# A four-layer diffusion trunk on one core: sublayer ends in two parts of feature quarters, weight conversions on VectorE, three tiles handed over

## The chip, the cores and the metric

The kernel runs on one core of one Trainium2 chip. The metric is the device time of one execution in microseconds (us), as the median of three runs. All traces are of that one core.

The core's engines work side by side, each through its own list of instructions in a fixed order: TensorE (PE: matrix products and transposes; its weight loads are shown as PEld), VectorE (DVE), ScalarE (ACT), GpSimd (POOL) and SyncE (SP, which issues most transfers). An instruction waits for the semaphores of what it reads and writes; everything behind it on its engine waits with it.

## What is computed

Four layers, each a token mixer (differential attention `da`, neighbourhood attention `na`, grouped-query attention `gq`, Hyena convolution `hy`) and a squared-ReLU MLP. After each of these eight sublayers the residual stream is updated, normalised and modulated for the next one:

```python
def layer_norm(x, g, b):
    xf = x.astype(jnp.float32)
    mu = jnp.mean(xf, axis=-1, keepdims=True)
    var = jnp.mean(jnp.square(xf - mu), axis=-1, keepdims=True)
    return ((xf - mu) * lax.rsqrt(var + LN_EPS) * g + b).astype(x.dtype)

def modulate(x, shift, scale):
    return x * (1.0 + scale) + shift
```

A sublayer adds `gate * (o @ w)` to ALPHA times the stream, applies `layer_norm`, and hands `modulate(...)` of it to the next. There are 128 context tokens and 512 latent tokens, 1024 features, all in float32.

## The kernel before

The 640 tokens are five tiles of 128: tile 0 holds the context, tiles 1 to 4 the latents. Products are made in three passes (`mm3`): a float32 operand is split into a high part `hh` or `hl[:, 0]` that TensorE takes at its fast rate and a low part (`hl`), and high x high, high x low and low x high are added up. So each weight of 128 x 1024 is converted after it arrives: a cast on ACT (L451) and a subtraction (L453) on DVE. Converted weights live in five buffers, raw ones in three; `wget` takes the next one of the stream and keeps the conversion a given number ahead.

The change is about the seven **ends** at which a sublayer passes over into the next (`sublayer_end`; the eighth, after the last MLP, has a branch of its own). An end has five tiles by four feature quarters of closing products, 20 groups of 12 matmuls of 128 x 256. Of each group DVE multiplies the result by the gate (`gtmp`, L655), and DVE or POOL adds it to the stream `r` (L662). When a tile has its four quarters, `ln_norm` takes statistics (two `bn_stats` L687, `bn_aggr` L689), the square root on ACT (L691), reciprocal and factor on DVE (L692, L693), and normalises the tile on ACT (L698; half of tile 4 on DVE, L700). `ln_out` then transposes it on TensorE (8 transposes L724 into `lnt`) and makes the next sublayer's input: the first half of the features by four modulations on ACT (L730), the second by a multiplication and an addition on DVE (L732, L733), each then cast to `hh` on ACT (L734) and subtracted to `hl` (L736; on POOL for the first half of tiles below LT = 3, else DVE).

The order within an end: tile by tile, all four quarters of a tile one after the other, the norm of tile t - 1 between the two halves of tile t, and `ln_out` two tiles behind. The last two `ln_out` are left **pending**; the next sublayer begins with products on tiles already made and calls `flush` between them (the MLP's `w1_first` after each of its first four products of 256 tokens; the mixers' `lead`, which takes two query and key projections and then the values; `hy_in_gen`). Thereafter `settle` scales the residual stream (L742, L743 on POOL and DVE). The four closing weights must all be there from the start of an end, so those of the next sublayer are converted during it: one at tile 3, two at tile 4 and one behind. Of these three have their subtraction on POOL, since `relieve` is set from tile 4 until the last `flush`.

The order of the instructions on each engine follows a scheduler's priorities, except where `manual_schedule` keeps the order in which the code is written.

Of the kernel before, what the change touches and what calls it, by code (L numbers as in the profile page):

```python
# [18 lines left out]
P = 128  # L19
D = 1024  # L20
# [37 lines left out]
LT = 3  # L58
# [13 lines left out]
# ---------------------------------------------------------------- host layout and shape constants  # L72
# [206 lines left out]
# ---------------------------------------------------------------- device program  # L279
class Trunk:  # L280
# [4 lines left out]
    def __init__(self, ctx, tc, a, outs, layers):  # L285
# [13 lines left out]
        self.relieve = False  # L299
# [9 lines left out]
        self.early = {}  # L309

    # ---- small helpers
# [33 lines left out]
    # ---- weight stream  # L345
# [28 lines left out]
    def side_keys(self, n):  # L374
        """filter work of the MLP of the layer at n: entries after each unit of w1, and after each of w2"""
# [19 lines left out]
    def head_order(l):  # L395
        """order of the projections: values of a group of four heads, queries and keys of a pair"""
# [39 lines left out]
    def w_convert(self, upto):  # L436
        while self.w_cv < min(upto, len(self.wlist)):
# [34 lines left out]
    # ---- products in three passes  # L472
# [6 lines left out]
    def span_a(self, ps, t, c0, c1):  # L479
        """feature-major product of one unit with tokens c0 to c1; yields now and then"""  # L480
# [6 lines left out]
    # ---- adaLN  # L487
# [30 lines left out]
    def ada_load(self, l, step):  # L518
        """weights of one step: 128 rows (or the bias row) of two neighbouring modulations"""
# [10 lines left out]
    def ada_step(self, raw, l, m, k):  # L530
        """128 rows of a modulation weight times their factors, added up row by row; the sum over partitions ends it"""
# [39 lines left out]
    def ada_gen(self, l, ahead, p0, p1):  # L571
        """pairs p0 to p1 of modulations of a layer; one step per yield, its weights loaded `ahead` steps before"""
# [44 lines left out]
    def load_ln(self, l, j, last=False):  # L617
        """gain and bias of a LayerNorm on all partitions, scaled for the residual stream"""
# [9 lines left out]
    def spill(self):  # L628
        """residual stream to DRAM, to be fetched by restore"""
# [13 lines left out]
    def restore(self):  # L643
        """residual stream back on chip; its tiles are finished by ready"""
# [4 lines left out]
    def residual(self, ps, t, q, quick=False):  # L649
        """r[t, quarter q] += gate * ps"""  # L650
# [13 lines left out]
    # ---- LayerNorm and modulation  # L664
# [80 lines left out]
    def ln_residual(self):  # L745
        for t in range(NT):
            self.ln_tile(t)
# [1482 lines left out]
```

## Time and profile before

| | us |
|---|---|
| median of 3 runs (1 core) | 3496.15 |
| the three runs | 3494.53, 3496.15, 3499.4 |
| span of the profiled execution | 3487.9 |
| busy PE / DVE / ACT / POOL | 3324.3 / 2600.0 / 1512.3 / 1003.6 |

The profiled execution is, by its span, 8.2 us shorter than the median of the runs. A row of a timeline gives start, duration, engine, line, operation and tile names, and in brackets how long the engine was idle before it and what ended that. A row of stretches gives each engine's busy time and, under PEclk, the TensorE clock that was granted, as a share of full speed. Matmul rows are pipelined, so a row's length is more than its share of the time.

### The profile page before, as it was taken

The page shows a single profiled execution, that of the slowest core. Times are in us where ns is not written, and L with a number is a line of the kernel's source. Part 1 is how long each engine was busy: PE and PEld are TensorE (multiplying, and loading weights), DVE is VectorE, ACT ScalarE, POOL GpSimd, SP SyncE. Part 2 cuts the span into 40 slices and gives each one's busy share as a digit, 9 for nine tenths or more (in the row PEclk, how much of TensorE's full clock was granted, in tenths as well). Part 3 has the DMA queues.
Part 4 walks back from the last instruction along what each step waited for, and adds up shares of the span by engine and source line. Part 5 has one row for each costly group of instructions (what it writes and reads, how often), then busy time and mean ns, then how long its engine had stood idle before and what let it go on. Part 6 is the DMA issues. An engine that isn't in the chain of part 4 may idle for free. (4 is left out here: it accounts for less than half of the span.)

```text
span 3487.9 us, 63715 instructions
## 1 busy us (share of the span) xinstructions
PE 3324.3 (95%) x25288; PEld 3183.9 (91%) x25288; DVE 2600.0 (75%) x4691; ACT 1512.3 (43%) x2700; POOL 1003.6 (29%) x961
## 2 busy tenths in 40 slices
PE   8998999999999989999998999999998999999998
PEld 6878889998999889999988889999998998999998
DVE  4777888788676678777688878777859888945457
ACT  3555453333356654433335665333324333432322
POOL 0333334334354453122252014232334112500002
PEclk9999999999999999999999999999999999999999
DMA  7343134545242324555412112545523224222221
GB/s 271 122 133 108 49 129 165 171 166 175 82 130 77 104 75 158 187 169 197 143 60 69 31 53 94 184 152 182 164 93 123 81 81 152 88 91 79 85 75 54
DMA packets 157644, 418.97 MB, mean 120 GB/s; under 512 B 19550, under 2 KB 29414, under 8 KB 154270
## 3 DMA queue, kind: packets, MB, share of 16 engines
q1 hardware_dynamic: 157344, 414.88, 35.8%
q8 instruction: 199, 3.26, 0.4%
q14 instruction: 101, 0.83, 0.1%
HBM read 371.20 MB, written 34.05 MB: 116 GB/s over the span
## 5 line engine op out<-in xcount | busy, mean ns | idle before, releaser
L662 POOL TENSOR_TENSOR r<-r,gtmp 128x256 f32<-128x256 f32 x444 | 437.8, 999 | 1127.6 <-DVE gtmp L655 1097.3
L453 DVE TENSOR_TENSOR hl<-raw,hl 128x1024 fp32r<-128x1024 f32 x390 | 506.6, 1301 | 322.1 <-ACT hl L451 320.6
L475 PE MATMUL w<-hl,ff 128*128 128x256 f32 x2560 | 716.0, 280 | 7.2 <-DVE gtmp L655 7.1
L476 PE MATMUL w<-hl,ff 128*128 128x256 f32 x2560 | 715.2, 279 | 2.5 <-DVE hl L453 2.4
L477 PE MATMUL w<-hl,ff 128*128 128x256 f32 x2560 | 713.9, 279 | 0.0
L451 ACT CAST hl<-raw 128x1024 fp32r<-128x1024 f32 x411 | 430.2, 1048 | 638.3 <-PE w L477 508.9
L475 PE MATMUL w<-hh,hl 128*128 128x320 f32 (+2 forms) x2048 | 637.7, 312 | 0.2
L476 PE MATMUL w<-hl,hl 128*128 128x320 f32 (+2 forms) x2048 | 634.9, 310 | 1.8 <-DVE hl L736 1.8
L477 PE MATMUL w<-hh,hl 128*128 128x320 f32 (+2 forms) x2048 | 634.3, 310 | 0.0
L475 PEld LDWEIGHTS w<-hl,ff 128*128 128x128 f32 x2560 | 481.0, 188 | 12.1 <-DVE gtmp L655 9.9
L476 PEld LDWEIGHTS w<-hl,ff 128*128 128x128 f32 x2560 | 480.9, 188 | 5.0 <-DVE hl L453 3.3
L477 PEld LDWEIGHTS w<-hl,ff 128*128 128x128 f32 x2560 | 479.9, 187 | 0.0
L543 DVE SCALAR_TENSOR_TENSOR ada<-adaw,sil,ada 128x512 f32<-128x512 f32 x504 | 388.2, 802 | 88.2 <-DMA adaw<-in_ada_w 80.5
L475 PEld LDWEIGHTS w<-hh,hl 128*128 128x128 f32 x2048 | 387.2, 189 | 13.8 <-issue 8.4
L476 PEld LDWEIGHTS w<-hl,hl 128*128 128x128 f32 x2048 | 387.2, 189 | 3.1 <-DVE hl L736 3.0
L477 PEld LDWEIGHTS w<-hh,hl 128*128 128x128 f32 x2048 | 387.0, 189 | 0.8 <-issue 0.8
L655 DVE TENSOR_TENSOR gtmp<-w,gate 128x256 f32<-128x256 f32 x640 | 261.1, 415 | 162.4 <-PE w L477 152.1
L874 ACT ACTIVATE fx<-w 128x640 f32<-128x640 f32 (+2 forms) x136 | 91.6, 673 | 454.2 <-PE w L477 435.3
L475 PE MATMUL qk<-hh,hl 128*128 128x320 f32 (+2 forms) x672 | 216.5, 322 | 6.7 <-DVE gtmp L655 3.9
L476 PE MATMUL qk<-hl,hl 128*128 128x320 f32 (+2 forms) x672 | 211.0, 314 | 0.0
L477 PE MATMUL qk<-hh,hl 128*128 128x320 f32 (+2 forms) x672 | 211.0, 314 | 0.0
L475 PE MATMUL wo<-hl,oh 128*128 128x256 f32 x640 | 184.0, 288 | 8.9 <-DVE gtmp L655 5.8
(344 smaller groups left out, 7132.4 us busy)
## 6 DMA issues: line engine op xcount, KB each, us to landing
raw<-in_w SPq DMA_DIRECT2D x256, 512.0 KB
adaw<-in_ada_w SPq DMA_DIRECT2D x288, 256.0 KB
adaw<-in_ada_w SPq DMA_DIRECT2D x16, 1024.0 KB
raw<-ab_d SPq DMA_DIRECT2D x32, 512.0 KB
raw<-in_hy_in SPq DMA_DIRECT2D x24, 512.0 KB
adaw<-in_ada_s SPq DMA_DIRECT2D x8, 1024.0 KB
raw<-in_da_qk SPq DMA_DIRECT2D x16, 512.0 KB
gate<-gate_d SPq DMA_DIRECT2D x32, 256.0 KB
```

What stands on the lines that cost most here:

```text
L451: self.nc.scalar.copy(t[:, 0], raw)
L453: sub(t[:, 1], raw, t[:, 0].bitcast(F32))
L475: mm(ps, w[0], x[0], start=start, stop=False)
L476: mm(ps, w[0], x[1], start=False, stop=False)
L477: mm(ps, w[1], x[0], start=False, stop=stop)
L543: nc.vector.scalar_tensor_tensor(out=y, in0=raw[h], scalar=x, in1=y, op0=ALU.mult, op1=ALU.add)
L655: nc.vector.tensor_mul(tmp, ps, self.gate[2 * s + q // 2][:, (q % 2) * 256:(q % 2) * 256 + 256])
L662: eng.tensor_add(rv, rv, tmp)
L874: nc.scalar.activation(x, src, AF.Relu)
```

## The change

`sublayer_end` gets the next weight by a function (`unit`), one quarter at a time, and works in two parts. Part 1 goes quarter by quarter: quarter 0 for all five tiles, then quarter 1 for all five, where the statistics of a tile's first half (`ln_half`) follow. The weights of the coming quarters and of the next sublayer are converted meanwhile, up to four ahead. Part 2 goes tile by tile through quarters 2 and 3, with each tile's norm right behind it; `ln_out` of tiles 0 and 1 follows tiles 2 and 3; three tiles stay pending in place of two. From part 2 to `settle`, PE and POOL keep the written order. The conversions' subtractions are always on DVE, the first half of tile 2 is subtracted on DVE (LT = 2), the second half of each tile is modulated by four instructions of 128 x 128 in place of two of 128 x 512, and the residual stream is scaled from tile 4 on. `lead` hands over after its first, second and third product; the Hyena opening hands over a third time. In `gq`, four multiplications for the rotary tables go from DVE ahead of the opening to ACT behind it. Docstrings fall away. The core of the diff:

```diff
-LT = 3
+LT = 2
@@ w_convert
-            sub = self.nc.gpsimd.tensor_sub if self.relieve else self.nc.vector.tensor_sub
-            sub(t[:, 1], raw, t[:, 0].bitcast(F32))
+            self.nc.vector.tensor_sub(t[:, 1], raw, t[:, 0].bitcast(F32))
@@ ln_norm
+            st = self.st.pop(t) if t in self.st else self.ln_half(t, 0)
+            self.ln_half(t, 1, st)
@@ ln_out
-                nc.vector.tensor_mul(x, pss[h], self.gs[:, f, s:s + 1].to_broadcast([P, 4, P]))
-                nc.vector.tensor_add(x, x, self.bs[:, f, s:s + 1].to_broadcast([P, 4, P]))
+                for k in range(4):
+                    nc.vector.tensor_scalar(out=x[:, k], in0=pss[h][:, k], scalar1=self.gs[:, 4 + k, s:s + 1], scalar2=self.bs[:, 4 + k, s:s + 1], op0=ALU.mult, op1=ALU.add)
@@ ln_residual
-        for t in range(NT):
+        for t in (NT - 1,) + tuple(range(NT - 1)):
@@ sublayer_end
-        for t in range(NT):
-            group(t, 0)
-            if t == 1:
-                while self.ln_raw:
...
-            if t == 3:
-                self.w_convert(self.wi + 1)
-            if t == NT - 1:
-                self.relieve = True
-                self.w_convert(self.wi + 3)
-            if t > 0:
-                self.ln_norm(t - 1)
-            group(t, 1)
-            if t == NT - 1:
-                self.ln_norm(t)
-            if t > 1:
+        self.st = {}
+        for q in range(2):
+            u = unit(q, 4)
+            for t in range(NT):
+                group(u, t, q, False)
...
+                if q == 1:
+                    self.st[t] = self.ln_half(t, 0)
+        self.man.enter_context(self.tc.manual_schedule(engines={mybir.EngineType.PE, mybir.EngineType.Pool}))
+        us = {2: unit(2, 4)}
+        us[3] = unit(3, 3)
+        for t in range(NT):
+            for q in (2, 3):
+                group(us[q], t, q, t > 2)
+            self.ln_norm(t)
+            if t in (2, 3):
                 self.ln_out(t - 2)
         self.w_convert(self.wi + 4)
-        self.pending = [lambda t=t: self.ln_out(t) for t in (NT - 2, NT - 1)]
+        self.pending = [lambda t=t: self.ln_out(t) for t in range(2, NT)]
@@ v_gen
-            if led and t > 2:
+            if led and t > 1:
@@ lead
-        for g in tiles + [None, None, values]:
+        for g in (tiles[0], None, tiles[1], None, values, None):
@@ gq
-                    nc.vector.tensor_scalar(out=t[s], in0=cs[s], scalar1=gg[:, 2 * i + s:2 * i + s + 1], scalar2=None, op0=ALU.mult)
...
             self.lead(ks, values)
+                    nc.scalar.activation(t[s], cs[s], AF.Copy, scale=gg[:, 2 * i + s:2 * i + s + 1])
@@ hy_in_gen
                     yield from self.span_a(early[1], early[0], c0, c1)
+                    self.flush(1)
```

The last argument of `group` puts the additions to `r` on DVE: before for tile 4, now for tiles 3 and 4.

Where instructions come to stand is shown at the first end (`da` to its MLP). Names carry numbers: `r_3495` is the stream, `gtmp` a gated product, `st`, `mv` and `rs` the statistics, the mean and variance and the factors of one tile, `hl_` with `raw_` a weight. **VectorE at the first norms.** Before, `mv_4305` and `rs_4307` are of tile 0 and `st_4376` is of tile 1:

```order
L655 TENSOR_TENSOR gtmp_4263<-wo_4250,gate_3716 128x256
L662 TENSOR_TENSOR r_3495<-r_3495,gtmp_4263 128x256
L687 BN_STATS st_4302<-r_3495 128x6
L655 TENSOR_TENSOR gtmp_4279<-wo_4266,gate_3503 128x256
L689 BN_AGGR mv_4305<-st_4302 128x2
L655 TENSOR_TENSOR gtmp_4295<-wo_4282,gate_3503 128x256
L687 BN_STATS st_4376<-r_3495 128x6
L692 RECIPROCAL rs_4307<-rs_4307 128x1
L655 TENSOR_TENSOR gtmp_4325<-wo_4312,gate_3718 128x256
L693 SCALAR_TENSOR_TENSOR rs_4307<-mv_4305,rs_4307 128x1
```

Now `st_4307` and `rs_4423` are of tile 0, `st_4325` is of tile 1, `hl_4383` is a weight of the next sublayer:

```order
L452 TENSOR_TENSOR hl_4383<-raw_4198,hl_4383 128x1024
L654 TENSOR_TENSOR gtmp_4401<-w_4388,gate_3716 128x256
L654 TENSOR_TENSOR gtmp_4417<-w_4404,gate_3716 128x256
L661 TENSOR_TENSOR r_3495<-r_3495,gtmp_4417 128x256
L683 BN_STATS st_4307<-r_3495 128x6
L654 TENSOR_TENSOR gtmp_4441<-w_4428,gate_3718 128x256
L698 BN_AGGR mv_4421<-st_4307 128x2
L654 TENSOR_TENSOR gtmp_4457<-w_4444,gate_3718 128x256
L683 BN_STATS st_4325<-r_3495 128x6
L701 RECIPROCAL rs_4423<-rs_4423 128x1
L654 TENSOR_TENSOR gtmp_4481<-w_4468,gate_3718 128x256
L702 SCALAR_TENSOR_TENSOR rs_4423<-mv_4421,rs_4423 128x1
```

In both the reciprocal of tile 0 stands behind statistics of tile 1: before behind those of its first half, now behind those of its last quarters; a weight's subtraction stands ahead of the first gated product of part 2.

**ScalarE at the end of the last tile.** Before, `rs_4579` is of tile 3, `rs_4621` of tile 4, `h_4524` and `h_4531` are the halves of tile 1, `h_4637` and `h_4644` those of tile 2:

```order
L698 ACTIVATE r_3495<-r_3495,rs_4477 128x1024
L730 ACTIVATE h_4524<-lnt_4514,bs,gs 128x128 x4
L734 CAST hh_4200<-h_4524 128x4x128
L451 CAST hl_4568<-raw_4188 128x1024
L734 CAST hh_4200<-h_4531 128x4x128
L451 CAST hl_4571<-raw_4190 128x1024
L691 ACTIVATE rs_4579<-mv_4577,epst 128x1
L451 CAST hl_4649<-raw_4195 128x1024
L698 ACTIVATE r_3495<-r_3495,rs_4579 128x1024
L730 ACTIVATE h_4637<-lnt_4627,bs,gs 128x128 x4
L451 CAST hl_4786<-raw_4658 128x1024
L691 ACTIVATE rs_4621<-mv_4619,epst 128x1
```

Now `h_4582` and `h_4589` are the halves of tile 1, `h_4518` the first half of tile 0, `rs_4503` is of tile 2, `rs_4567` of tile 3:

```order
L707 ACTIVATE r_3495<-r_3495,rs_4503 128x1024
L743 CAST hh_4189<-h_4518 128x4x128
L739 ACTIVATE h_4582<-lnt_4572,bs,gs 128x128 x3
L700 ACTIVATE rs_4567<-mv_4565,epst 128x1
L739 ACTIVATE h_4582<-lnt_4572,bs,gs 128x128
L451 CAST hl_4637<-raw_4200 128x1024
L707 ACTIVATE r_3495<-r_3495,rs_4567 128x1024
L743 CAST hh_4189<-h_4582 128x4x128
L743 CAST hh_4189<-h_4589 128x4x128
L451 CAST hl_4798<-raw_4289 128x1024
L700 ACTIVATE rs_4631<-mv_4629,epst 128x1
L707 ACTIVATE r_3495<-r_3495,rs_4631 128x512
```

Four casts of weights stood here and two do now; the first of them and the norm of tile 3 stand between tile 1's modulation and its cast.

**GpSimd over the same stretch.** Before, the last two additions and what follows them:

```order
L662 TENSOR_TENSOR r_3495<-r_3495,gtmp_4495 128x256
L736 TENSOR_TENSOR hl_4201<-h_4524,hh_4200 128x4x128
L453 TENSOR_TENSOR hl_4568<-raw_4188,hl_4568 128x1024
L453 TENSOR_TENSOR hl_4571<-raw_4190,hl_4571 128x1024
L736 TENSOR_TENSOR hl_4201<-h_4637,hh_4200 128x4x128
L453 TENSOR_TENSOR hl_4649<-raw_4195,hl_4649 128x1024
L742 TENSOR_TENSOR r_3495<-r_3495,ln_g_4110 128x512
```

Now:

```order
L661 TENSOR_TENSOR r_3495<-r_3495,gtmp_4481 128x256
L745 TENSOR_TENSOR hl_4190<-h_4518,hh_4189 128x4x128
L745 TENSOR_TENSOR hl_4190<-h_4582,hh_4189 128x4x128
L751 TENSOR_TENSOR r_3495<-r_3495,ln_g_4110 128x512
L752 TENSOR_TENSOR r_3495<-r_3495,ln_b_4112 128x512
```

The three subtractions of weights and the one of tile 2 are gone.

## Rows read from the trace of the kernel before

**Rows 1.** The page's first part: busy time, share of the span, instructions of each engine.

```profile
PE 3324.3 (95%) x25288; PEld 3183.9 (91%) x25288; DVE 2600.0 (75%) x4691; ACT 1512.3 (43%) x2700; POOL 1003.6 (29%) x961
```

**Rows 2.** Stretches of 52 us, one around each end: length, busy times, granted clock, DMA.

```profile
418.00:470.00 52.00, 46.25 (x345) 45.17 (x344) 47.48 (x68) 31.76 (x57) 35.02 (x25) 0.93 0.17 52
...
1775.00:1827.00 52.00, 43.78 (x331) 42.30 (x331) 47.18 (x70) 24.80 (x48) 33.96 (x25) 0.90 0.17 58
...
2989.00:3041.00 52.00, 46.11 (x345) 44.84 (x344) 47.94 (x68) 29.31 (x53) 34.79 (x25) 0.93 0.12 42
sum 364.00, PE 317.63 PEld 308.80 DVE 330.88 ACT 201.24 POOL 244.43; mean PE 45.38 PEld 44.11 DVE 47.27 ACT 28.75 POOL 34.92
```

**Rows 3.** Waits of PE from 418 to 470: total us, times, longest.

```profile
PE lnt L724 <- ACT r L698: 5.0, 2, 4.4
```

**Rows 4.** Waits of PE from 1775 to 1827, the end of the second MLP.

```profile
PE v L475 <- DVE h L732: 2.6, 1, 2.6
PE qk L475 <- DVE rs L693: 2.5, 1, 2.5
```

**Rows 5.** Timeline of PE at the first end; x8 are eight transposes.

```profile
425.76 1.03 PE L724 MATMUL lnt<-ident,r 128*128 128x128 f32 x8
...
432.29 1.03 PE L724 MATMUL lnt<-ident,r 128*128 128x128 f32 x8
433.15 0.38 PE L475 MATMUL wo<-hl,oh 128*128 128x256 f32 x1
...
452.90 1.97 PE L724 MATMUL lnt<-ident,r 128*128 128x128 f32 x8 [4.42 <-ACT r L698]
```

**Rows 6.** Short stretches behind a PE gap at the first and fourth end.

```profile
452.00:456.00 4.00, 3.10 (x15) 3.11 (x16) 4.00 (x4) 2.57 (x5) 3.92 (x3) 0.52 0.77 230
456.00:460.00 4.00, 4.00 (x24) 4.00 (x24) 3.97 (x4) 2.22 (x6) 3.84 (x4) 0.63 0.11 38
...
1800.00:1804.00 4.00, 3.13 (x15) 3.16 (x16) 3.93 (x12) 3.11 (x6) 0.00 (x0) 0.57 0.80 282
```

**Rows 7.** Timeline of DVE at the first end.

```profile
415.94 0.42 DVE L662 TENSOR_TENSOR r<-r,gtmp 128x256 f32<-128x256 f32 x1
...
419.03 0.69 DVE L687 BATCH_NORM_STATS2 st<-r 128x6 f32<-128x512 f32 x1 [1.13 <-POOL r L662]
...
437.39 2.18 DVE L662 TENSOR_TENSOR r<-r,gtmp 128x256 f32<-128x256 f32 x1
...
446.87 1.23 DVE L453 TENSOR_TENSOR hl<-raw,hl 128x1024 fp32r<-128x1024 f32 x1
```

**Rows 8.** Timeline of POOL at the first end.

```profile
433.17 0.74 POOL L662 TENSOR_TENSOR r<-r,gtmp 128x256 f32<-128x256 f32 x1 [1.13 <-DVE gtmp L655]
435.17 1.31 POOL L736 TENSOR_TENSOR hl<-h,hh 128x512 fp32r<-128x512 f32 x1 [1.26 <-ACT hh L734]
436.44 5.38 POOL L453 TENSOR_TENSOR hl<-raw,hl 128x1024 fp32r<-128x1024 f32 x2
...
447.61 1.62 POOL L736 TENSOR_TENSOR hl<-h,hh 128x512 fp32r<-128x512 f32 x1 [5.79 <-ACT hh L734]
```

**Rows 9.** Timeline of ACT at the first end.

```profile
423.25 1.25 ACT L698 ACTIVATE r<-r,rs 128x1024 f32<-128x1024 f32 x1 [0.49 <-DVE rs L693]
426.40 1.51 ACT L730 ACTIVATE h<-lnt,bs,gs 128x128 f32<-128x128 f32 x4 [1.90 <-PE lnt L724]
427.94 0.62 ACT L734 CAST hh<-h 128x512 fp32r<-128x512 f32 x1
...
437.58 1.04 ACT L451 CAST hl<-raw 128x1024 fp32r<-128x1024 f32 x1
```

**Rows 10.** Groups by line and form, whole span: busy us, mean ns of one, idle before.

```profile
L453 POOL TENSOR_TENSOR hl<-raw,hl 128x1024 fp32r<-128x1024 f32 x21 | 56.3, 2693 | 0.0
...
L733 DVE TENSOR_TENSOR h<-h,bs 128x512 f32<-128x512 f32 x35 | 37.2, 1064 | 0.3
...
L732 DVE TENSOR_TENSOR h<-lnt,gs 128x512 f32<-128x512 f32 x35 | 23.6, 676 | 1.0 <-PE lnt L724 1.0
```

More of the change, by code (lines that the diff above doesn't have):

```diff
@@ L683, in ln_norm @@
         r = self.r[:, t]
-        n = 4 if last else 2
-        st = (self.small(12, "st") if n == 2 else self.S(F32, "st", 24)).rearrange("p (a b) -> p a b", a=n)
-        for h in range(n):
-            nc.vector.bn_stats(st[:, h], r[:, h * D // n:(h + 1) * D // n])
+        if last:
+            st = self.S(F32, "st", 24).rearrange("p (a b) -> p a b", a=4)
+            for h in range(4):
+                nc.vector.bn_stats(st[:, h], r[:, h * 256:(h + 1) * 256])
+        else:
+            st = self.st.pop(t) if t in self.st else self.ln_half(t, 0)
+            self.ln_half(t, 1, st)
         mv = self.small(2, "mv")
@@ L768, in settle, with sublayer_end @@
                 p()
-    def sublayer_end(self, l, j, group, last=False, spill=False):
+    def sublayer_end(self, l, j, unit, group, last=False, spill=False):
         if last:
+            us = [unit(q, 1) for q in range(4)]
             for t in range(NT):
-                group(t, 0)
-                group(t, 1)
+                for q in range(4):
+                    group(us[q], t, q, t == NT - 1)
                 self.ln_norm(t, t == NT - 1)
@@ L834, in out_steps @@
         for q in range(4):
-            u = {q: self.wget((nm + "_o", q), ahead=1)}
+            u = self.wget((nm + "_o", q), ahead=1)
             if q == 1:
@@ L842, in out_steps @@
                     split(oh, 0, t + 2)
[L843 removed]
+                self.quarter(u, oh, t, q)
                 self.out_left -= 1
@@ L859, in out_rest @@
             pass
-        units = [self.wget((nm + "_o", 4 + q), ahead=1) for q in range(4)]
-        self.sublayer_end(l, 0, lambda t, i: self.out_group(units, oh, t, (2 * i, 2 * i + 1), t == NT - 1))
+        self.sublayer_end(l, 0, lambda q, ahead: self.wget((nm + "_o", 4 + q), ahead), lambda u, t, q, quick: self.quarter(u, oh, t, q, quick))
     def mlp(self, l, nxt, last):
@@ L907, in w1_first @@
             self.settle()
-        def w2_group(u, ch, q, t, quick=False):
-            ps = self.any1([P, 256], "w2")
-            c = slice(t * P, (t + 1) * P)
-            for kk in range(4):
-                f = slice(kk * 256, (kk + 1) * 256)
-                self.mm3(ps, (ff[ch][:, 0, kk, c], ff[ch][:, 1, kk, c]), (u[:, 0, f], u[:, 1, f]), kk == 0, kk == 3)
-            self.residual(ps, t, q, quick)
         for ch in range(8):
@@ L930, in mlp @@
                 for t in range(NT):
-                    w2_group(u, ch - 1, q, t)
+                    self.quarter(u, ff[ch - 1], t, q)
                     groups += 1
@@ L937, in mlp @@
             self.tap_step()
-        units = [self.wget(("w2", l, 28 + q), ahead=1) for q in range(4)]
-        def close(t, i):
-            for q in (2 * i, 2 * i + 1):
-                w2_group(units[q], 7, q, t, t == NT - 1)
-        self.sublayer_end(l, 1, close, last, nxt in (1, 3))
+        self.sublayer_end(l, 1, lambda q, ahead: self.wget(("w2", l, 28 + q), ahead), lambda u, t, q, quick: self.quarter(u, ff[7], t, q, quick), last, nxt in (1, 3))
     def v_gen(self, nm, gr, vv, chunks, state):
@@ L1414, in mixer_gq @@
             self.lead(ks, values)
+            for i in (1, 0):
+                t = [self.S(F32, f"tab{i}{s}") for s in range(2)]
+                for s in range(2):
+                    nc.scalar.activation(t[s], cs[s], AF.Copy, scale=gg[:, 2 * i + s:2 * i + s + 1])
+                tab[i] = t
             for i, x in enumerate(xk):
```

31 lines of the change are left out of this document (14 added, 17 removed).

## The prediction

> **What bounds the kernel now.** I read the page's busy times first: TensorE works 3324.3 of 3487.9 us [rows 1]; no other engine passes 75%. So an edit pays only if it closes one of PE's idle times, 163.6 us in all, or gives back clock. Then I cut a stretch of 52 us around each of the seven ends. Over 364.00 us PE is busy 317.63, so it idles 46.4 us there [rows 2], 28% of all its idle time in a tenth of the span. The same rows give the clock: in the seven stretches it was granted at .90 to .97 of full speed, and the shortfalls add up to .47 x 52 = 24.4 us, the most that the half clock can cost there. The short stretches tell where it falls: behind a gap of 4.42 us at the first end it stands at 0.52 for 4 us and at 0.63 for 4 more [rows 5, 6], the 1.2 GHz level for most of it. PE was busy 3.10 and 4.00 of these, so 3.10 x .48 + 4.00 x .37 = 3.0 us were lost, against .07 x 52 = 3.6 by the share. With the same ratio the seven ends lose 24.4 x 3.0/3.6 = 20 us. **What this change can touch is 46 + 20 = 66 us.**
>
> Who ends the waits: at the first end PE waits 5.0 us for ACT's norm, 4.4 of it at once [rows 3, 5]; at the fourth for the factors and for a modulated half, 2.5 and 2.6 [rows 4]. These are chains through DVE, ACT and POOL behind the last tiles, and the DVE rows tell why they are late. An addition that takes 0.42 us takes 2.18 while POOL works on weight subtractions (5.38 for two) [rows 7, 8]. There are 21 of these, three at each of seven ends, 56.3 us [rows 10].
>
> **The change, part by part.** PE's own work stays: the same 20 groups of 12 matmuls and 5 x 8 transposes per end. From [rows 5], 48 matmuls and 8 transposes take 432.29 - 425.76 = 6.53 us and the 8 transposes 433.15 - 432.29 = 0.86, so a group takes 1.42 us. The times below count from the start of part 2 at the first end. PE ends tile 0 at 2.8, tile 1 at 5.7, tile 2 at 8.5, and would then transpose tile 0.
>
> Removed: POOL's three weight subtractions. The DVE instructions beside them come back to their own length, some 5 us of DVE time per end (1.8 for the addition named and its like). This does not shorten PE by itself; it decides when the chain of tiles 3 and 4 is ready. The 4.4 us gap in front of the fourth tile's transposes goes, since now nothing blocks DVE between statistics and factors, and since a product of the next sublayer now stands between each two hand-overs.
>
> Added on DVE: the same subtractions at 1.23 us each [rows 7], all but one in part 1, where PE has 10 groups (14 us) that need no norm; this work is hidden. One stands at the head of part 2: it ends at 4.4, so tile 0's two gated products leave DVE only at about 4.7, the addition at 5.5, the second statistics (0.69) at 6.0. If part 1 ran late on DVE, each 1.23 us of it would appear in front of tile 0's transposes.
>
> **The first new wait** is the place in DVE's order where the reciprocal of tile 0 stands behind the statistics of tile 1. Those wait for POOL's additions (0.74 each [rows 8]; such a wait stands in the trace at 1.13 us [rows 7]); the last of tile 1 is done at about 7.8 and the statistics at 8.5. Reciprocal and factor are out at 9.5, ACT normalises for 1.25 [rows 9] and is done at 11.0. PE waits from 8.5 to 11.0: **2.5 us**. Queued behind are tile 3's products, so nothing fills it.
>
> **The second** is at the end. PE ends tile 4 at 18.5 and needs both parts of tile 1 for the opening. ACT is busy without a break from 11.7: modulations at 1.51 per half tile, casts at 0.62, the norms of tiles 1, 2 and 3 at 1.25, and one weight's cast (1.04) [rows 9]. That cast cannot start before PE has ended quarter 2 of tile 4, since its buffer is that quarter's weight; it stands ahead of tile 3's norm and tile 1's cast. The high part of tile 1 is ready at 20.9, the low part on POOL (1.31 [rows 8]) at 22.1. PE waits 2.4 us for its first product and 1.2 for its second, **3.7 in all**. In the MLP's opening only one product then covers tile 4's chain: 1.1 us more. Sum 2.5 + 3.7 + 1.1 = 7.2. So at the ends behind `da`, the first MLP, `na` and `gq`; in `na`'s opening the last part is 1.7 + 0.6 in place of 1.1, so 8.5: 3 x 7.2 + 8.5 = 30.1.
>
> At the other three the reciprocal stands right behind its own statistics. The same working gives 0.7 and 0.9 us in front of the transposes of tiles 0 and 1, 1.0 for tile 2's and 0.4 + 1.2 in the opening, 4.2; in front of `gq` and `hy` 2.1 more for tile 4, whose input the second halves of the opening products wait for. 4.2 + 2 x 6.3 = 16.8. **Idle after: 30.1 + 16.8 = 47, as before (46.4).** The same hand working on the old order gives 0.3, 0.7, 0.8 and 4.4 us at the first end, against 4.4 + 0.6 for the norms in the trace [rows 3]. A tenth more per hand-over between engines would raise the sum to 53; at the least, if ACT never stands in the way, only the wait for the norm of a tile that PE has just ended (2.6 at four ends, 1.8 at three) and some 2 us in each of three mixers are left, about 22.
>
> **The clock** is where I see a gain. A gap of 2.5 us cost 4 us at 0.57 [rows 4, 6], 4.00 x .43 = 1.7; the 4.4 us gap cost 3.0. Now the gaps are 2.5 and 2.4 + 1.2. What PE loses behind the first it need not wait for at the second, which ends by ACT: the weight's cast has 1.1 us of room there, so 0.6 of 1.7 remain. Behind the second, tile 4's wait of 1.1 takes as much: again 0.6. So 1.2 at four ends, 4.8; and 1.7 behind the last wait in each of the three mixers, 5.1; none behind gaps under 1.3 us. Together 10 in place of 20. **Sum: 47 + 10 = 57 against 66, 9 us less.**
>
> A rule of the Trainium skill speaks against the moved subtractions. [Rows 7] show DVE blocked while POOL runs. By the page "SBUF — State Buffer", section "SBUF: two separate sides", the pair of ports is an exclusive lock held for a whole instruction by whichever of the two engines starts first, a DVE operation with two SBUF inputs included. The trace agrees for DVE; for POOL, which by the rule would be held up as long, it shows no more than a cast of 1.31 to 1.62 us [rows 8]. What that would make of the time is in the first rival.
>
> The rest: four modulations of 128 x 128 for a multiplication and an addition (0.68 + 1.06 [rows 10]) lie off the path except at tile 4; between nothing and those 1.7 us per end if they cost nothing at all, and since four starts are paid for two I take nothing. Tile 2's cast on DVE for POOL is 0.6 to 0.7 us beside PE's wait for ACT: nothing. The order of the residual scaling and the `gq` tables on ACT: both beside products that wait for nothing of theirs. SP's loads keep their order but for a few that move ahead; the buffers come free with PE's quarters, 14 us earlier for the first two, so no transfer is later.
>
> **The rivals.** *The waits and the clock cost what they did*: the POOL lock was the cost before, its end bought only the two new queues on DVE and ACT, and each half-clock stretch is paid in full: gap 1.7 + gap 1.7 at four ends is 13.6, with 5.1 in mixers 18.7 for 20. Then 47 + 19 = 66: 3496. Or a weight's subtraction on DVE (1.23 [rows 7]) holds up POOL's last cast once at each end, 7 x 1.2 = 8 us of my 9: 3495. For it: idle is the same by my own sum.
>
> *Slower:* at four ends two gaps take the place of one. If each falls into the clock like the 4.4 us gap (0.52 and 0.63 over 8 us, 3.4 us by the share) and none of it is hidden, they cost 4 x 2 x 3.4 = 27; the mixers' 5 and 5 for the three other ends make 37, 17 more than now: 3513. It decides once the clock's loss in the ends passes 20 us with idle time as now. For it: every gap of over 2 us that I looked at had such a stretch behind it. Against: the shorter ones had 1.7.
>
> *Much faster:* ACT and DVE, free of the lock, are ahead of my hand schedule and only the structural waits remain: 22 + 10 = 32 for 66, 3462.
>
> *It does not do what it says:* "conversions ahead" holds for three of four units; the fourth, bound by its buffer, is in the forecast.
>
> **How the numbers follow.** The terms are against the profiled execution (3487.9, 8.2 below the median); I carry the difference of 9 over to the median: 3496.15 - 9 = **3487 us**, own range 3479 (0.2% around the idle sum, one wait per end less) to 3493 (idle 53). Forecast 50%; same cost 24%; slower 16%; much faster 10%. The range takes in the slower rival down to 3508 and the faster one to 3462. A measurement of this kernel tells 0.2% (7 us) from no change: under 3489.2 is faster. Of the forecast's 50% I put 37 there and 13 within; of the same cost 3 there, 19 within and 2 above. Faster 37 + 10 + 3 = 0.50, within 0.2% 13 + 19 = 0.32, slower 16 + 2 = 0.18.
>
> **What would show it.** In the profile after: PE's wait for the norm in front of tile 0's transposes, 2.5 us at four ends and 0.7 at three, with the reciprocal behind tile 1's statistics in DVE's timeline; the first product behind tile 4 waiting 2.4 us for the cast and 1.2 for POOL's, with the weight's cast ahead on ACT; idle in the seven ends 47; clock in them above .96; no DVE operation of the ends over 1.3 us beside POOL. I am wrong if PE's first wait is above 4 us (DVE late out of part 1), if the clock falls twice per end to 0.55, or if waits grow where I counted nothing, in the mixers' openings or in part 1.

## The result, and the profile after

The changed kernel takes 3518.45 us, the median of four runs (3513.22 to 3520.29), against 3496.8 for the kernel before on the same chip: ratio 1.0066, 95% interval [1.0054, 1.0078]. It is 22 us slower. The forecast was 3487 and the range ended at 3508. The page's first lines, to be held against [rows 1]:

```profile
span 3518.3 us, 63781 instructions
PE 3334.1 (95%) x25288; PEld 3187.6 (91%) x25288; DVE 2582.8 (73%) x4785; ACT 1512.8 (43%) x2704; POOL 931.4 (26%) x933
```

POOL works 72 us less and DVE 17 less, as the change meant; PE works 10 us longer on the same 25288 matmuls, which is where a lower clock would show (granted over the whole span it is 0.986 before and 0.985 now); the rest of the 30 us between the two spans is idle time, 20.6.

To see where, I cut both traces at the same points of the program: each stretch begins with an end's first closing product and is 580 PE instructions long, so it holds the end and the opening behind it. The stretches of after (length, busy times, clock; the columns of [rows 2]):

```profile
412.01:502.68 90.67, 81.86 (x582) 80.31 (x581) 70.17 (x123) 45.25 (x79) 27.41 (x24) 0.94 0.27 88
934.68:1022.77 88.09, 77.91 (x583) 76.30 (x582) 67.17 (x116) 38.35 (x73) 35.60 (x37) 0.96 0.29 92
1278.99:1368.94 89.95, 80.84 (x583) 79.40 (x582) 68.34 (x116) 45.93 (x79) 27.48 (x25) 0.96 0.28 94
1792.33:1880.60 88.27, 78.26 (x583) 76.22 (x582) 66.19 (x138) 40.57 (x77) 34.12 (x30) 0.94 0.20 62
2122.64:2213.01 90.37, 81.06 (x583) 79.62 (x581) 69.51 (x118) 45.68 (x79) 28.49 (x26) 0.96 0.28 89
2628.77:2722.99 94.22, 82.06 (x583) 78.35 (x581) 81.34 (x161) 42.10 (x81) 29.60 (x28) 0.93 0.28 95
3011.66:3096.28 84.62, 79.25 (x582) 76.88 (x581) 65.45 (x113) 43.25 (x76) 27.97 (x26) 1.00 0.28 88
sum 626.19, PE 561.24 PEld 547.07 DVE 488.17 ACT 301.13 POOL 210.68; mean PE 80.18 PEld 78.15 DVE 69.74 ACT 43.02 POOL 30.10
```

The same cut of before, one line for the sum:

```profile
sum 604.14, PE 554.02 PEld 542.01 DVE 508.82 ACT 305.01 POOL 280.68; mean PE 79.15 PEld 77.43 DVE 72.69 ACT 43.57 POOL 40.10
```

| end | before: length, idle, clock | after: length, idle, clock | longer by |
|---|---|---|---|
| da to MLP | 86.34, 5.81, .96 | 90.67, 8.81, .94 | 4.3 |
| MLP to na | 81.13, 5.37, .98 | 88.09, 10.18, .96 | 7.0 |
| na to MLP | 85.82, 6.16, .96 | 89.95, 9.11, .96 | 4.1 |
| MLP to gq | 85.66, 8.37, .94 | 88.27, 10.01, .94 | 2.6 |
| gq to MLP | 85.55, 6.77, .98 | 90.37, 9.31, .96 | 4.8 |
| MLP to hy | 93.18, 11.75, .95 | 94.22, 12.16, .93 | 1.0 |
| hy to MLP | 86.46, 5.89, .96 | 84.62, 5.37, 1.00 | -1.8 |
| sum | 604.1, 50.1 | 626.2, 65.0 | 22.0 |

The ends carry all of the 22 us, and the four ends at which the reciprocal stands behind tile 1's statistics carry 20.2 of them. I call them the four ends below, and the others the three. (The two profiled spans differ by 30.4; the other 8 lie between the ends, where the instructions stand as before but for some at the edges of the stretches and in `gq` behind its opening. A second profile of the changed kernel, `a_again`, has them at 4.)

Most of it is idle time: 14.8 of the 22.0 us here, and 7.2 are longer work of PE. In `a_again` the same seven stretches are 19.1 us longer than before, 16.6 of it idle and 2.5 work:

```profile
sum 623.27, PE 556.53 PEld 542.45 DVE 487.08 ACT 301.51 POOL 210.72; mean PE 79.50 PEld 77.49 DVE 69.58 ACT 43.07 POOL 30.10
```

PE's waits at the first end of after:

```profile
437.24 1.11 PE L733 MATMUL lnt<-ident,r 128*128 128x128 f32 x8 [2.46 <-ACT r L707]
449.12 0.58 PE L474 MATMUL w<-hh,hl 128*128 128x256 f32 x1 [2.71 <-ACT hh L743]
450.83 0.58 PE L475 MATMUL w<-hl,hl 128*128 128x256 f32 x1 [1.13 <-POOL hl L745]
```

So the 4.42 us gap of [rows 5] is gone, and two stand in its place, where the prediction put them. The first comes from DVE. Statistics of tile 1 that wait for POOL, and then the reciprocal and the factor of tile 0 behind them:

```profile
434.71 0.69 DVE L683 BATCH_NORM_STATS2 st<-r 128x6 f32<-128x512 f32 x1 [1.13 <-POOL r L661]
435.32 0.15 DVE L701 RECIPROCAL rs<-rs 128x1 f32<-128x1 f32 x1
435.38 0.41 DVE L654 TENSOR_TENSOR gtmp<-w,gate 128x256 f32<-128x256 f32 x1
435.70 0.15 DVE L702 SCALAR_TENSOR_TENSOR rs<-mv,rs 128x1 f32<-128x1 f32 x1
```

The second comes from ACT's queue. Tile 1's first half is modulated in two parts (x3 and x1), with tile 3's square root between them, then come the weight's cast and tile 3's norm, and only then the two casts that PE waits for:

```profile
443.66 1.15 ACT L739 ACTIVATE h<-lnt,bs,gs 128x128 f32<-128x128 f32 x3
445.84 0.29 ACT L700 ACTIVATE rs<-mv,epst 128x1 f32<-128x1 f32 x1 [1.03 <-DVE mv L698]
446.04 0.44 ACT L739 ACTIVATE h<-lnt,bs,gs 128x128 f32<-128x128 f32 x1
446.38 1.03 ACT L451 CAST hl<-raw 128x1024 fp32r<-128x1024 f32 x1
447.32 1.24 ACT L707 ACTIVATE r<-r,rs 128x1024 f32<-128x1024 f32 x1
448.46 1.13 ACT L743 CAST hh<-h 128x512 fp32r<-128x512 f32 x2
```

And the clock behind both gaps of the third end, in stretches of 5 us:

```profile
1305.00:1310.00 5.00, 5.00 (x32) 5.00 (x31) 2.88 (x12) 3.96 (x8) 0.00 (x0) 0.66 0.00 0
1316.00:1321.00 5.00, 3.19 (x16) 3.00 (x17) 4.64 (x6) 2.19 (x4) 1.63 (x1) 0.78 0.35 108
```

Behind the first gap PE is busy for the whole 5 us and loses 5 x .34 = 1.7 us; behind the second it falls again.

One end shows what the first of these stretches does to the second gap. In `a_again`, the same kernel once more, the first end has the same first gap, but the clock behind it stays at full speed:

```profile
437.82 1.09 PE L733 MATMUL lnt<-ident,r 128*128 128x128 f32 x8 [2.46 <-ACT r L707]
447.72 0.39 PE L474 MATMUL w<-hh,hl 128*128 128x256 f32 x1 [2.27 <-ACT hh L743]
```

```profile
438.00:443.00 5.00, 5.00 (x45) 5.00 (x45) 4.36 (x15) 4.48 (x9) 0.00 (x0) 1.00 0.02 5
```

```profile
444.43 0.31 ACT L700 ACTIVATE rs<-mv,epst 128x1 f32<-128x1 f32 x1
```

Tile 3's square root comes without the wait of 1.03 us, the second gap is 2.27 us for 2.71, and from tile 0's transposes to the opening's first product 9.90 us pass where it was 11.88. This first gap is the only one of the eight in the two profiles without a half-clock stretch behind it; why it has none, the rows do not show.

### The profile page after: what moved, and what is told of

The parts are those of the page before. It is cut to its first block, busy times and chain, and to the rows that moved or that the text cites. A ratio compares the mean times of both kernels' runs of the same rounds, so it can differ in the third digit from the quotient of the medians.

```text
span 3518.3 us, 63781 instructions
## 1 busy us (share of the span) xinstructions
PE 3334.1 (95%) x25288; PEld 3187.6 (91%) x25288; DVE 2582.8 (73%) x4785; ACT 1512.8 (43%) x2704; POOL 931.4 (26%) x933
## 4 chain that ended last, share of the span: by engine, by line
PE 57%; DVE 13%; issue 3%; ACT 3%; POOL 2%; DMA 1%; DVEq 0%; SPq 0%; POOLq 0%; ACTq 0%
PE w L474 13%; PE w L475 13%; PE w L476 13%; DVE hl L452 2%; PE ptp L1059 2%; PE pv L2053 2%; DVE gtmp L654 2%; PE s L2006 1%; PE qk L475 1%; PE qk L474 1%; PE qk L476 1%; DVE ada L542 1%; PE py L1769 1%; DVE r L661 1%; DVE st L683 1%
## 5 line engine op out<-in xcount | busy, mean ns | idle before, releaser
L452 DVE TENSOR_TENSOR hl<-raw,hl 128x1024 fp32r<-128x1024 f32 x411 | 535.0, 1305 | 326.7 <-ACT hl L451 325.5
L474 PEld LDWEIGHTS w<-hl,ff 128*128 128x128 f32 x2560 | 481.2, 188 | 16.9 <-DVE gtmp L654 14.8
L654 DVE TENSOR_TENSOR gtmp<-w,gate 128x256 f32<-128x256 f32 x800 | 325.8, 415 | 190.4 <-PE w L476 173.5
L474 PE MATMUL w<-hl,oh 128*128 128x256 f32 x640 | 186.5, 292 | 9.7 <-DVE gtmp L654 6.5
```

Source lines behind the costliest of these rows:

```text
L452: self.nc.vector.tensor_sub(t[:, 1], raw, t[:, 0].bitcast(F32))
L474: mm(ps, w[0], x[0], start=start, stop=False)
L654: nc.vector.tensor_mul(tmp, ps, self.gate[2 * s + q // 2][:, (q % 2) * 256:(q % 2) * 256 + 256])
```

## The experiments

Theory A: the loss sits at the four ends, in the two queues (DVE's and ACT's), and each of the two gaps costs a half-clock stretch of its own. Theory B: the first gap does not matter, since the second ends later anyway and gives back what is lost. All ratios are to the kernel before on the same chip; "four" and "three" are the summed lengths of the stretches above. The kernels ran on several chips, and the kernel before differs by 5 us between them, so where two kernels ran on different chips I give the difference by the ratios beside that of the medians.

| kernel | median us | ratio [95%] | four | three |
|---|---|---|---|---|
| before | 3491.8 to 3496.8 | 1 | 338.8 | 265.3 |
| changed | 3518.45 | 1.0066 [1.0054, 1.0078] | 359.1 | 267.1 |
| a_again | 3516.03 | 1.0060 [1.0045, 1.0075] | 356.3 | 267.0 |
| e1_recip | 3486.72 | 0.9981 [0.9971, 0.9990] | 332.1 | 268.5 |
| e2_hold | 3503.66 | 1.0033 [1.0022, 1.0045] | 346.0 | 267.9 |
| e3_both | 3481.27 | 0.9966 [0.9953, 0.9979] | 324.5 | 266.7 |
| e4_fill | 3492.26 | 1.0001 [0.9991, 1.0010] | | |
| e5_fill4 | 3515.28 | 1.0061 [1.0046, 1.0076] | | |
| e6_fill20 | 3493.07 | 1.0005 [0.9995, 1.0014] | | |
| e9_fill8 | 3501.28 | 1.0019 [1.0010, 1.0029] | | |
| e10_fill16 | 3491.59 | 0.9991 [0.9982, 1.0000] | | |
| e12_held_fill | 3509.63 | 1.0036 [1.0024, 1.0049] | 350.0 | 267.9 |
| e13_held_fill2 | 3501.30 | 1.0012 [1.0002, 1.0021] | 344.0 | 268.5 |
| e14_held_recip | 3502.67 | 1.0018 [1.0008, 1.0027] | 344.2 | 267.9 |
| e7_before_dve | 3501.97 | 1.0024 [1.0014, 1.0034] | 348.5 | 266.1 |
| e8_lead | 3471.31 | 0.9936 [0.9920, 0.9953] | 321.0 | 260.2 |
| e11_early4 | 3468.28 | 0.9927 [0.9911, 0.9944] | 322.3 | 258.6 |

**The two queues.** e1_recip orders DVE:

```diff
-            self.ln_half(t, 1, st)
+            if t:
+                with self.tc.issue_after(self.rs_i.ins):
+                    self.ln_half(t, 1, st)
...
-        nc.vector.scalar_tensor_tensor(out=rs[:, 1:2], ...
+        self.rs_i = nc.vector.scalar_tensor_tensor(out=rs[:, 1:2], ...
```

> The changed kernel with one order more: at each end the last statistics of a tile are queued on DVE behind the factor of the tile before, so that at the four ends after da, the first MLP, na and gq the reciprocal of tile 0 no longer stands behind the statistics of tile 1. Theory A (two queues at these four ends carry the loss, each gap with its own half-clock stretch): the 2.5 to 2.7 us gap in front of tile 0's transposes falls to the 0.8 us that the other three ends show, its half-clock stretch (3.4 us at 1.2 GHz, 1.7 lost) goes with it, 4 x 3.5 less: about 3505. Theory B (the gap only moves, since tile 1's casts set the opening): PE reaches the opening earlier and waits there as much longer; 3515 to 3519.

3486.7, 32 us less than the changed kernel (30 by the ratios): twice theory A's gain. Whether B is out, this run does not tell, since the second gap went too (below). The four stretches lose 27 us (359.1 to 332.1), the three are as they were. e2_hold orders ACT:

```diff
-        self.w_convert(self.wi + 4)
+        with self.tc.issue_after(self.last_act.ins):
+            self.w_convert(self.wi + 4)
```

(`last_act` is the latest cast of `ln_out`.)

> The changed kernel with the conversion of the fourth weight queued on ACT behind tile 1's last cast to hh. Theory A: the opening's wait of 2.7 to 3.1 us behind tile 4 falls by the cast's 1.0 us at the four ends, with a little less of half clock, 4 to 7 us in all: about 3513. Theory B (other work sets the opening: tile 3's norm, PE's own slow stretch before it): under 2 us, 3517 to 3520; if the held weight is then late for the fourth product of the opening, a new wait of 1 to 2 us there.

3503.7, 15 less (12 by the ratios) where 4 to 7 were expected. The edge brought tile 1's first cast ahead of tile 3's norm (1.24 us) as well, and PE's wait behind tile 4 fell from 2.7 to 3.1 us to 0.5 to 1.2. ACT in e2_hold:

```profile
445.14 0.62 ACT L743 CAST hh<-h 128x512 fp32r<-128x512 f32 x1
445.67 1.24 ACT L707 ACTIVATE r<-r,rs 128x1024 f32<-128x1024 f32 x1
```

Both together:

> Both orders of e1_recip and e2_hold. Theory A: the four ends become like the other three, which lost 2 us together against before; of the 20 us that the four lost nearly all comes back, 3497 to 3502. Theory B: 3510 or above, with the opening's wait at 3 to 4 us.

3481.3, faster than the kernel before by 0.34%. The four ends now take 324.5 us against 338.8 before. PE and POOL execute the changed kernel's order at every place, so what made the change slow lies in the order of DVE and ACT. How few places of it would do, these three runs do not show, since each edge moved more than it names: against the changed kernel e1_recip differs at 90 of 4785 places on DVE and 38 of 2704 on ACT, e2_hold at 59 and 46, e3_both at 182 and 117.

Why more than expected? In e1_recip the edit touches DVE, but the scheduler then laid ACT out anew too: as in e2_hold, the first cast of tile 1 now stands ahead of the weight's cast and of tile 3's norm, and the four modulations are in one piece. ACT in e1_recip:

```profile
437.86 1.50 ACT L743 ACTIVATE h<-lnt,bs,gs 128x128 f32<-128x128 f32 x4
439.24 0.30 ACT L704 ACTIVATE rs<-mv,epst 128x1 f32<-128x1 f32 x1
439.42 0.62 ACT L747 CAST hh<-h 128x512 fp32r<-128x512 f32 x1
439.93 1.06 ACT L451 CAST hl<-raw 128x1024 fp32r<-128x1024 f32 x1
```

Two causes, the first gap and the second, moved at once, and they had to be taken apart.

**Filling the gap.** The first try puts work that nothing needs into PE's first gap at the four ends, so that only PE's busy time changes:

```diff
+        if fill:
+            for k in range(24):
+                nc.tensor.transpose(pss[0][:, k % 4], self.ident, self.ident)
         for k in range(KD):
             nc.tensor.transpose(pss[k // 4][:, k % 4], self.r[:, t, k * P:(k + 1) * P], self.ident)
```

> The changed kernel with 24 transposes of the identity (about 2.5 us of work that nothing needs, written over by what follows) in front of tile 0's transposes at the four ends where PE idles 2.5 to 2.7 us. The gap is the same for everything behind it; only PE is busy in it. If the half clock behind this gap costs time: no 1.2 GHz stretch there, tile 3's products run 1.7 us shorter at each of the four, 3511. If what is lost behind the first gap is given back at the second, as the prediction held (all but 0.6): 3516 to 3518.

3492.3: useless work made the kernel some 23 us faster. But its trace shows DVE and ACT in another order than the changed kernel, so this is clock and order at once. The pairs with 4 and 20, and 8 and 16 fillers were to hold the order:

> Since e4_fill also came out in another order on DVE and ACT, this and e6_fill20 are a pair: the changed kernel with 4 filler transposes in front of tile 0's transposes at the four ends (about 0.4 us of work), 20 (about 2.1 us) in e6_fill20, and the same order of every instruction on DVE and ACT in both. Here PE still idles about 2 us in front of tile 0. Theory A (the half clock behind the first gap costs time of its own and makes the second gap longer): a 1.2 GHz stretch behind this gap at the four ends, and 7 to 14 us more than e6_fill20. Rival (what is lost behind the first gap is given back at the second): the two within 3 us of each other.

> The other one of the pair: 20 filler transposes, all else as in e5_fill4. PE is busy in nearly all of the first gap. Theory A: no 1.2 GHz stretch at the four ends, near e4_fill's 3492. Rival: within 3 us of e5_fill4.

> e6_fill20 had turned out in another order on DVE and ACT than e5_fill4, so that pair did not hold order fixed as its text says. This one and e10_fill16 do: the same order of all instructions on DVE and ACT (listed and compared before the run), 8 filler transposes here (about 0.9 us), 16 there (about 1.7 us), in front of tile 0's transposes at the four ends. PE idles some 1.8 us there in this one and 0.9 us in the other. If the half clock behind the first gap costs time by itself: a 1.2 GHz stretch here and none there, 1.7 us or more at each of four ends, 7 to 14 us more than e10_fill16. If the order alone made e6_fill20 fast: within 2 us of e10_fill16. If no 1.2 GHz stretch follows 1.8 us of idleness either, the two are equal and the pair says only that.

> 16 filler transposes, the order of e9_fill8 on DVE and ACT. Near e6_fill20 (3493), no 1.2 GHz stretch at the four ends.

They don't, against what the last two texts say of it. By the executed traces e5_fill4 stands exactly in the order of the changed kernel, e6_fill20 does not, and e9_fill8 and e10_fill16 differ from each other at 123 of 4785 places on DVE and 94 of 2704 on ACT. The 22 and 10 us between the pairs are therefore inconclusive as to the clock. In e9_fill8 and e10_fill16 the 5 us behind the first gap stand at 1.00 at all four ends, so the 10 us between them cannot be a half-clock stretch there. What e5_fill4 does say: with the order unchanged and the gap still 2.0 to 2.2 us, nothing is gained (3515.3).

**Held orders.** The last three kernels tie DVE and ACT to the changed kernel's order by an edge from each instruction of part 2 and of the hand-overs to the one behind it; their traces show the order of the changed kernel at every place on both engines (e14_held_recip but for the move):

```diff
+            for a, b in zip(want, want[1:]):
+                self.tc.add_manual_dep(mine[b], mine[a].name, mybir.DependencyInfo(mybir.DependencyClass.NoSync, mybir.DependencyReason.DATA), reason="order")
```

> The changed kernel with 24 filler transposes in front of tile 0's transposes at the four ends, as e4_fill, but with every instruction of DVE and ACT from the second part of an end to the end of the hand-over held in the order of the changed kernel by explicit edges. Only TensorE's busy time in the first gap differs. If the half clock behind this gap costs time by itself: no 1.2 GHz stretch in tile 3's products, about 1.7 us less at each of four ends, 3508 to 3512. If it is given back at the second gap: 3514 to 3519. If e4_fill's 3492 comes back, the clock alone carried all of it and the order nothing.

3509.6, 6 us less than a_again (8 by the ratios), as theory A said. PE at the third end of e12_held_fill, filler first:

```profile
1294.06 2.78 PE L744 MATMUL lnt<-ident 128*128 128x128 f32 x24
1296.88 1.09 PE L746 MATMUL lnt<-ident,r 128*128 128x128 f32 x8
...
1306.78 0.38 PE L484 MATMUL w<-hh,hl 128*128 128x256 f32 x1 [2.27 <-ACT hh L756]
```

and its clock behind the filled gap:

```profile
1298.00:1303.00 5.00, 5.00 (x45) 5.00 (x45) 4.48 (x14) 5.00 (x11) 0.36 (x1) 1.00 0.00 0
```

Full speed where the changed kernel had 0.66. The second gap is not longer for it but shorter: 2.27 us against 2.89 at this end of the changed kernel, whose ACT chain had waited for products of tile 3 that ran at half speed (2.27 to 2.38 at the four ends, against 2.71 to 3.09). From tile 0's transposes to the opening's first product it is 9.90 us, as at the one full-speed end of a_again. So the loss behind the first gap was not given back; it was passed on. e13_held_fill2 fills the second gap too (20 transposes into the opening's first PSUM tile):

> As e12_held_fill, with 20 filler transposes (2.1 us) more in front of the opening's first product at the same ends, in the second gap. If the half clock behind the second gap costs time too: another 1.7 us at each of four ends, 3501 to 3506. If the wait for tile 4 behind it takes it up: as e12_held_fill; if the filler is longer than the gap that is left, up to 4 us more than e12_held_fill.

3501.3, again 8 us less, and again as A said. The clock behind its second gap:

```profile
1302.80:1306.50 3.70, 3.70 (x34) 3.70 (x34) 3.12 (x8) 1.10 (x3) 0.00 (x0) 1.00 0.42 151
```

Nothing was taken off DVE or ACT and their order is the same; only PE's products run faster, and what hangs on them comes sooner. Against a_again this brings 15 us (17 by the ratios, 12 in the four stretches). **The half clock behind the two gaps costs 12 to 17 us at the four ends.** That is its price, and not what it adds to the kernel before: by length times shortfall of the clock the four stretches lose 16 us in the changed kernel, 1.7 in e13_held_fill2 and 10 in the kernel before.

> The changed kernel with the reciprocal and the factor of tile 0 moved ahead of tile 1's last statistics at the four ends, and everything else on DVE and ACT held in the order of the changed kernel. Theory: the first gap falls from 2.7 to 0.8 us and its half clock goes, 4 x (1.9 + 1.7) = 14 us less, 3502 to 3505; the rest of e1_recip's gain, some 17 us, was the order that the scheduler then gave ACT. Rival: the reciprocal alone carries it, 3486 to 3490.

3502.7, as A said: the reciprocal's place alone is worth 13 us against a_again (15 by the ratios), gap and clock together. B, by which the second gap would have taken up what the first lost, is out: the second gap is 2.4 us at all four ends, where the changed kernel's profile has 2.7 to 3.1. The other 16 us of e1_recip's gain (13 by the ratios) came with the rest of its new order, which closed the second gap; most of that is ACT's, but DVE's differs further too (90 places, of which the move is 16). In e14_held_recip, with ACT in the old order, the second gap stands:

```profile
1289.97 1.09 PE L743 MATMUL lnt<-ident,r 128*128 128x128 f32 x8 [0.81 <-ACT r L717]
...
1300.53 0.39 PE L484 MATMUL w<-hh,hl 128*128 128x256 f32 x1 [2.44 <-ACT hh L753]
```

In e1_recip the same product waits a fifth of that:

```profile
1290.76 0.38 PE L474 MATMUL w<-hh,hl 128*128 128x256 f32 x1 [0.49 <-ACT hh L747]
```

> The changed kernel unchanged, for its time and trace on the same chip as its variants: 3513 to 3520, of which the stretches around the seven ends account for 20 to 24 us over the kernel before, nearly all at the four ends after da, the first MLP, na and gq.

3516.0, as expected; the stretches account for 19 us, just under the 20 to 24 expected, and the four ends again carry it, 356.3 for 338.8.

**One part of the change alone**, in the kernel before: `self.relieve = False`, so that all subtractions of weights are on DVE.

> The kernel before with one part of the change alone: the subtractions of the weights always on DVE, none on POOL; nothing else. Theory (POOL's subtractions blocked DVE, and the 4.4 us gap in front of tile 3's transposes is theirs): the DVE operations of 2 us and more go, and the gap falls to 1 to 2 us with its half clock, 7 ends x 2 to 4 less, 3470 to 3482. Rival (DVE's own 3 x 1.2 us of subtraction stand in the same chain in place of the blocking): the gap stays at 3 us or above, 3490 to 3497.

It is slower than before by 0.24%, above both ranges; the rival, no gain, is the nearer. The gap in front of tile 3's transposes does fall, from 4.5 to 2.5 us, where the rival had it stay, but a new and longer one opens at the first product that needs tile 4. PE's waits at the third end of e7_before_dve:

```profile
PE w L476 <- DVE hl L736: 5.9, 1, 5.9
PE lnt L724 <- ACT r L698: 2.5, 1, 2.5
```

and DVE ahead of it:

```profile
1312.17 1.75 DVE L733 TENSOR_TENSOR h<-h,bs 128x512 f32<-128x512 f32 x1
1313.84 2.28 DVE L453 TENSOR_TENSOR hl<-raw,hl 128x1024 fp32r<-128x1024 f32 x1
1316.05 3.45 DVE L736 TENSOR_TENSOR hl<-h,hh 128x512 fp32r<-128x512 f32 x2
```

A weight's subtraction now stands in this chain, as the rival had it, and it is long: 2.28 us where one takes 1.23 [rows 7]. The addition takes 1.06 us on the mean of the kernel before [rows 10] and 1.75 here. POOL is at the residual scaling meanwhile, in e7_before_dve without subtractions of weights ahead of it:

```profile
1302.09 1.72 POOL L742 TENSOR_TENSOR r<-r,ln_g 128x512 f32<-128x512 f32 x1
```

and in the kernel before behind the last of them:

```profile
1299.85 2.78 POOL L453 TENSOR_TENSOR hl<-raw,hl 128x1024 fp32r<-128x1024 f32 x1
1302.59 1.27 POOL L742 TENSOR_TENSOR r<-r,ln_g 128x512 f32<-128x512 f32 x1
```

Counted from the start of the stretch the scaling begins at 38.1 us in place of 43.1. So POOL, relieved of one thing, begins the next one sooner, and DVE's work for tile 4 falls beside it. The Trainium skill's page "SBUF — State Buffer", section "SBUF: two separate sides", states an exclusive lock of the port pair that the two engines share, held for a whole instruction; these rows agree for DVE. How much of the new gap comes from the earlier scaling and how much from DVE's own subtractions, no run here separates.

**The openings.** e8_lead is e3_both with one line more:

```diff
-        for g in (tiles[0], None, tiles[1], None, values, None):
+        for g in (tiles[0], None, tiles[1], None, None, values):
```

> e3_both with one more order: in the openings of na and gq, lead hands over tiles 3 and 4 both ahead of the values' product, as the kernel before had it for its two, where the changed kernel hands over tile 4 behind it. Theory (nothing covers tile 4's chain there): the waits at the second halves of the first projections (1.4 + 0.6 in na, 2.4 + 1.2 in gq) and their half clock go, 4 to 8 us less than e3_both. Rival: tile 4's transposes wait for its norm ahead of the values instead, no change.

3471.3, 10 less than e3_both by the medians and by the ratios, and 10 in the stretches (591.2 to 581.2), 8.8 of it at the ends in front of `na` and `gq`. PE's waits at the gq end of the changed kernel:

```profile
PE qk L474 <- ACT hh L743: 2.4, 1, 2.4
PE qk L475 <- DVE hl L745: 1.2, 1, 1.2
```

In e8_lead they are gone, and one of 1.9 at the values is the longest:

```profile
PE v L474 <- DVE h L746: 1.9, 1, 1.9
```

e11_early4 hands over tiles 3 and 4 together in the MLPs and in hy as well (`self.flush(2 if len(self.pending) == 2 else 1)`):

> e8_lead with the last hand-over earlier in the MLPs and the Hyena opening too: tiles 3 and 4 both behind the second product, so that two products cover tile 4's chain in the MLPs and one in the Hyena opening. Theory: the waits for tile 4 at the second halves (0.7 to 1.8 us and 0.6 us in four MLPs, 2.0 + 1.7 in hy) shrink, 4 to 8 us less than e8_lead, 3464 to 3468. Rival: tile 4's transposes now wait for its norm, as before the change, no gain or a loss of up to 5 us.

3468.3; the stretches sum to 580.9 against 581.2, so of the expected 4 to 8 us nothing is to be seen there (the end in front of `hy` is 1.9 shorter, the others together 1.6 longer), and the 3 us between the medians are within the spread of the runs. It is by its median the fastest kernel of the study, 0.73% ahead of the kernel before, but not apart from e8_lead.

## Why the prediction was wrong

- **Where it is decided**: right. The ends carry the whole difference.
- **The first wait** (2.5 us at four ends, 0.7 at three): right, 2.46 to 2.67 and 0.81.
- **The second wait** (2.4 + 1.2): the place was right, the size 2.7 to 3.1 + 1.1 to 1.3. The step that ACT is "busy without a break" failed: it waits 1.03 us for tile 3's statistics, whose products ran at half clock. At the one end of a_again where they ran at full clock it does not wait, and the size was right too, 2.27 + 1.17.
- **Tile 4 in the openings** (1.1 in the MLPs, 1.7 + 0.6 in `na`): 1.58, and 0.6 to 0.9 more for an evacuation on ACT that the working had not followed; in `na` 1.36 + 0.63, and 1.1 for a weight's low part. Idle at the four ends 37.4 where 30.1 was worked out: 10.5 for the first wait, 16.9 for the second, 10.0 here.
- **The other three ends** (16.8): 27.5 in the longer stretches, where before has 26.0. In front of gq and hy tile 4's wait is 3.7 us (2.4 + 1.2, and 2.0 + 1.7) and not 2.1; e8_lead shows for gq that it is the order of `lead`, whose last hand-over has nothing behind it. A wait of 3.1 us for `rk` in gq, also new, was not followed further. The prediction had named waits in the mixers' openings that it had not counted as a sign of being wrong.
- **Idle in all** ("47, as before"): this step failed. It rose by 14.8 us (50.1 to 65.0), 13.3 at the four ends and 1.5 at the three; the working had 6 more at the four, paid back by 6 less at the three.
- **The clock** (10 in place of 20, the whole forecast gain): this step failed as much. By the rows it is 28 against 23.5 (length times shortfall), and 22.5 in a_again's trace: about as much as before in both. I had let each gap give back what the clock lost behind the other. e12_held_fill and e13_held_fill2 show the opposite: each half-clock stretch is paid in full, and the first also delays the chain that ends the second gap. Between 9 us less, as forecast, and 22 more lie 31 us: some 14 are idle time, and the rest is the longer work of PE, where the clock shows.
- **The rivals**: the one of unchanged cost had the clock right, each stretch paid in full and about as much as before, and the idle time as wrong as the forecast. The slower one had the mechanism, two gaps for one and each with its own stretch. Its price was made of too much clock (27 us for eight stretches, where filling both gaps brought 12 to 17) and no more idle time, where there are 15 us; so it stopped at 3513. "Much faster" is not this kernel; e3_both comes nearer to it, with waits of 1.4 us and less at the four ends.
- **The lock** (a subtraction on DVE holds up POOL's last cast, 8 us in the rival): POOL's cast beside DVE's subtraction took 1.63 us against 1.31 [rows 8], 0.3 and not 1.2, and none of the 14 such casts of the kernel took over 1.64. DVE's own low part behind it was 1.71 us long, so the sign "no DVE operation over 1.3 us beside POOL" failed. POOL, and then DVE:

```profile
449.14 1.63 POOL L745 TENSOR_TENSOR hl<-h,hh 128x512 fp32r<-128x512 f32 x1 [4.00 <-ACT hh L743]
```

```profile
448.42 1.21 DVE L452 TENSOR_TENSOR hl<-raw,hl 128x1024 fp32r<-128x1024 f32 x1
449.62 1.71 DVE L745 TENSOR_TENSOR hl<-h,hh 128x512 fp32r<-128x512 f32 x1
```

The lesson of method: the hand working had every instruction at its full-clock length and put the clock on top as a sum. Since the chain that ends the second gap begins in products of the first stretch, the clock belongs into the chain.

## What to carry to other kernels

Where a change replaces one long wait of TensorE by two (here 4.4 us by 2.5 and 2.7), count a half-clock stretch behind each (1.7 us here, behind seven of the eight first gaps) and run the chain behind it at that clock. When an engine's queue decides, look for the one instruction that stands behind another tile's work, as the reciprocal here: moving it was worth 13 us, and with ACT's queue in order as well the change that lost 22 us gained 12 (0.34%). Before taking a filler or an order edge as proof, compare the executed orders of all engines, since a scheduler answers one edit with many.

## What was not expected of the hardware

Filler in the first gap made the kernel faster by 6 us at a held order, and in both gaps by 15 (8 and 17 by the ratios): a busy TensorE was worth more here than an idle one even though nothing waits for what it does. The filler was transposes alone, and the clock behind them stood at 1.00. At the four ends of e1_recip, whose gaps are 0.5 to 1.6 us, the clock stood at 1.00 over three of the four stretches and at 0.98 over the fourth; behind the changed kernel's first gap it stood at 0.66.
